# Input projections of a hybrid-attention encoder: 512 columns at a time and weight parts in nine single tiles

## The chip, the cores and the metric

The kernel runs on one core of one Trainium2 chip. The metric is the device time of one execution in microseconds, from the first to the last instruction with what lies around it. Before the change three runs took 2704.49, 2706.41 and 2711.77 us (median 2706.41). Engine names are those of the profile: PE is TensorE (matmuls; PEld its weight loads), DVE is VectorE, ACT is ScalarE, POOL is GpSimd, SP is the engine whose queue issues the DMAs.

## The reference, cut to what matters

```python
D_MODEL = 1024; SEQ = 2048; HEAD_DIM = 64       # 8 + 8 heads, D_FF = 4096, all float32
def reference(x, c, g_norm1, w_in, g_q, g_k, rel_bias, w_o, g_norm2, w1, w2, w_ada, b_ada):
    ...
    mod = c_act @ w_ada[l] + b_ada[l]
    sh1, sc1, gt1, sh2, sc2, gt2 = [m[:, None, :] for m in jnp.split(mod, 6, axis=-1)]
    h = rmsnorm(x, g_norm1[l]) * (1.0 + sc1) + sh1
    proj = h @ w_in[l]
    q_sb, k_sb, v_sb, q_ca, k_ca, v_ca = jnp.split(proj, split_pts, axis=-1)
    ...
    q_ca = rmsnorm(hs(q_ca, N_CA_HEADS), g_q[l])
    k_ca = rmsnorm(hs(k_ca, N_CA_HEADS), g_k[l])
    ...
    x = x + gt1 * (mixed @ w_o[l])
    h = rmsnorm(x, g_norm2[l]) * (1.0 + sc2) + sh2
    x = x + gt2 * (jnp.square(jax.nn.relu(h @ w1[l])) @ w2[l])
```

The change lies in `proj = h @ w_in`: a product of 2048 x 1024 by 1024 x 3072. Its columns are six kinds of 512: q, k, v of the eight stick-breaking heads ("sb") and q, k, v of the eight chunked-attention heads ("ca"). The q and k of the second group also get an RMS norm over each head's 64 columns.

## The kernel before

Products in full precision are made of three fast ones: each operand is split in a high and a low part (`split`, line 146: ACT copies the high part, DVE or POOL subtracts it for the low part), and `mm3` (202) adds high x high, high x low and low x high. Tokens are taken in reverse, in four blocks of 512 (tb 3, 2, 1, 0).

The program has three stages. The first makes most of the projections, and on the side the 48 columns of `mod`, the prepared bias, and the split parts of w_o and of some of w_in, which it stores to DRAM for later. The second is the attention, into which the remaining projections and the output projection are filled. The third is the MLP, made of seven products per pair of blocks. Only the first is touched.

*Pieces and jobs.* w_in is cut into 12 pieces of 256 columns: 0 to 5 are q, k, v of sb, 6 to 11 those of ca. A job (f, piece, tb) is one piece for one block of tokens; its first number tells loads of the same piece apart. The list `jobs` (521 to 524) has 31. Pieces 0 to 3 use weights as the stationary operand and 512 tokens as the moving one (tiles `pq`): two blocks of 24 matmuls of 512 columns. The others use 128 tokens as the stationary operand and the 256 columns of the piece as the moving one (tiles `pt`): 96 matmuls in two blocks, a bank of PSUM holding two groups of 128 tokens. `project` (309) issues a job, and gives way after each block, so that `run_job` (535) can put side work behind it.

*Behind a block.* Values (pieces 4, 5, 10, 11) are split and stored. For q and k of ca, ACT squares the bank (`csq`), DVE sums per head (`cv`), POOL takes the inverse root (`rsqrt`, 150), and DVE multiplies the bank by it (`scale`, 346, writes `qh`), which frees the bank. When all four groups of 128 tokens are there, TensorE turns them (`turn`, 356, tiles `px`), and ACT and DVE split and store them.

*What sets the order.* TensorE always runs in program order; so do ACT, DVE, POOL and SP from job 7 on (`Ordered`, 34; `ORDERED`, 532), while up to there a scheduler orders these four. `Later` (57) holds closures that run a number of ticks later, one tick per block: `later` for `scale` and `turn`, `norms` for the three parts of a block's norm, `behind` for stores and the second halves of side work. Side work `todo` (527 to 530) has costs: 1.5 for a column of `mod` (`ada`: a load `wa` of 512 KB, two ticks later `ada_column` on DVE), 1.8 for a bias, 4.4 for a part of w_o (`prepare_wo`). Every block earns credit (573): 3.0 in early jobs of q, k of ca, 2.2 from job 7 on.

*Norms.* `start_norm(tb, wait)` (401) squares eight x tiles on ACT and adds them on DVE (`nsaa`); after `wait` ticks `norm_rstd` (171) makes eight small matmuls (`pva`), DVE `nva`, POOL the root, DVE `ndga`; some ticks later `norm_spread` makes `pra` and DVE scales x. `end_norm` (417) then makes the operand tiles `ht` of the block: per x tile two operations on ACT and one on DVE.

*Buffers.* PSUM banks come from `Banks` (253), which hands out in turn z, z, ps, z, z, ps: four buffers of tag z, two of tag ps. Raw weights come into `ring` (three of 8 KB a partition). Split weights lie in `wp` (251): two tiles `wh` and two `wl` of a whole piece, so a piece is split while the one before it is in use. `load_w` (281) splits with four pool subtractions per piece, in the ordered part at given points (`parts`). `stp` (250) has six staging tiles of 4 KB, `adaw` four for `wa`, `xp` ten x tiles.

Of the kernel before, what the change touches and what calls it, by code (L numbers as in the profile page):

```python
# [79 lines left out]
def encoder_kernel(ctx, tc, xT, c, g1, g2, w_in, gqk, bias, w_o, w1, w2, w_ada, b_ada, out):  # L80
# [127 lines left out]
    def store_qk(kind, ca, ps, pl, pair, tb, nm, g=None):  # L208
        st = pl.tile([P, 2, TB], F32R, tag="st", name=f"st{nm}")
# [27 lines left out]
    SBQK, CAQK, VALS = (2, 3, 0, 1), (6, 7, 8, 9), (4, 5, 10, 11)  # L237

    pa, er = ctx.enter_context(ExitStack()), ctx.enter_context(ExitStack())
    if True:
        xp = er.enter_context(tc.tile_pool(name="xp", bufs=KT + 2, side="right"))
        adaw = er.enter_context(tc.tile_pool(name="adaw", bufs=4, side="right"))
        adap = er.enter_context(tc.tile_pool(name="adap", bufs=1, side="right"))
# [4 lines left out]
        stp = pa.enter_context(tc.tile_pool(name="stp", bufs=6))  # L250
        wp = pa.enter_context(tc.tile_pool(name="wp", bufs=2))
# [3 lines left out]
        cb = adap.tile([P, D], F32, name="cb")  # L255
        cg = adap.tile([P, D], F32, name="cg")
# [8 lines left out]
        parts = []  # L265
# [10 lines left out]
        def load_raw(half, piece, q=None):  # L276
            wr = ring.tile([P, KT, CW], F32, tag="r8", name=f"wr{half}_{piece}")
            (q or sp).dma_start(wr, w_in[piece])
            return wr

        def load_w(half, piece, q=None, wr=None, parts=None):

            if wr is None:
                wr = load_raw(half, piece, q or sp)
            wh = wp.tile([P, KT, CW], F32R, tag="wh", name=f"wh{half}_{piece}")
            wl = wp.tile([P, KT, CW], F32R, tag="wl", name=f"wl{half}_{piece}")

            def low(k):
                pool.tensor_tensor(wl[:, k], wr[:, k], wh[:, k].bitcast(F32), op=ALU.subtract)

            for k in (slice(0, KT // 2), slice(KT // 2, KT)):
                act.copy(wh[:, k], wr[:, k])
                for kk in (slice(k.start, k.start + 2), slice(k.start + 2, k.stop)):
                    if parts is None:
                        low(kk)
                    else:
                        parts.append(lambda kk=kk: low(kk))
            if parts is not None:
                parts.append(lambda: behind.add(2, lambda: keep_w(half, piece, wh, wl)))
            elif q is None:  # L300
                keep_w(half, piece, wh, wl)
            return wh, wl

        def keep_w(half, piece, wh, wl):
            if half in (0, 2) and piece not in CAQK:
                for l, w in enumerate((wh, wl)):
                    sp.dma_start(scr_w[piece,][:, :, l, :], w.bitcast(F32))

        def project(piece, tb, ht, wh, wl):

            grp, hf = divmod(piece, 2)
            kind, ca = grp % 3, grp // 3
            nm = f"{piece}_{tb}"
            if not ca and kind < 2:
                for n in range(2):
                    ps = pp.tile([P, TB], F32, tag="ps", name=f"pq{nm}_{n}")
                    cl = slice(n * P, (n + 1) * P)
                    for k in range(KT):
                        mm3(ps, wh[:, k, cl], wl[:, k, cl], ht[k][:, 0, :], ht[k][:, 1, :], k == 0, k == KT - 1)
                    store_qk(kind, 0, ps, stp, hf * 2 + n, tb, f"{nm}_{n}")  # L320
                    yield
                return
            if kind < 2:
# [1284 lines left out]
```

## Time and profile before

| | before |
|---|---|
| median of three runs | 2706.41 us |
| profiled execution, its own time | 2706.24 us |
| its span, first to last instruction | 2704.4 us |
| instructions | 42721 |
| mean granted TensorE clock | 0.992 |
| 0 to 74 us: PE, DVE, ACT, POOL busy; DMA share | 51.9, 48.5, 40.1, 41.1 us; 0.93 |
| 436 to 1500 us | 1007.5, 857.3, 775.4, 645.7 us; 0.75 |
| 1500 to 2704 us | 1196.2, 798.6, 570.2, 206.0 us; 0.61 |

How to read it: rows of the timeline give the start in us, the length, the engine, the operation with its tiles (out<-in, numbers left out), the shape and how many were merged; in brackets stands the idle time before it and what ended that. Rows by stage give the length of the stretch, then for each engine its busy time and the number of instructions, the granted clock, the busy share of the DMA engines and GB/s. Rows of groups give busy time and the mean ns of one, then the idle time before them. L42 is the wrapper that keeps program order, so instructions are told apart by tile. Matmuls overlap: one lasts longer than the distance to the next, so their pace is read from starts.

### The profile page before, as it was taken

How to read it: one execution, taken by the hardware profiler on the slowest of the kernel's cores; microseconds unless marked ns; L12 is line 12 of the kernel's file. 1: busy time of each engine (PE TensorE's matmuls, PEld its weight loads, DVE VectorE, ACT ScalarE, POOL GpSimd, SP SyncE). 2: the span in 40 equal slices, each digit the busy share in tenths (PEclk: the TensorE clock that was granted, in tenths of full speed). 3: DMA queues.
4: the chain of work that ended last, by engine and by line, in shares of the span. 5: the costliest groups of instructions: out<-in, count | busy, mean ns of one | idle time of the engine just before them, and what ended most of it. 6: DMA issues, size and time to landing. Idle time of an engine off the chain costs nothing. (4 is left out here: it accounts for less than half of the span.)

```text
span 2704.4 us, 42721 instructions
## 1 busy us (share of the span) xinstructions
PE 2616.3 (97%) x14192; PEld 2231.1 (82%) x14192; DVE 1885.4 (70%) x3159; ACT 1516.7 (56%) x2926; POOL 1065.6 (39%) x1296
## 2 busy tenths in 40 slices
PE   6999999899999999999998999999999999999999
PEld 5899998778778987778876788878888888888887
DVE  6435555688789878989756777768866565655565
ACT  5423445687688878878643444455644444444443
POOL 5464365566466656767533323202001323200000
PEclk9999999999999999999999999999999999999999
DMA  9869977878888687756766876786675444465574
GB/s 341 314 253 341 379 276 232 259 245 256 267 258 245 210 262 250 231 190 207 215 227 215 283 265 254 266 334 210 230 265 186 150 152 152 148 238 190 202 265 156
DMA packets 265579, 650.36 MB, mean 240 GB/s; under 512 B 29200, under 2 KB 65040, under 8 KB 255632
## 3 DMA queue, kind: packets, MB, share of 16 engines
q1 hardware_dynamic: 264576, 645.55, 70.0%
q10 hardware_dynamic: 784, 2.10, 0.3%
q8 instruction: 112, 1.84, 0.3%
q14 instruction: 107, 0.88, 0.1%
HBM read 456.16 MB, written 191.37 MB: 239 GB/s over the span
## 5 line engine op out<-in xcount | busy, mean ns | idle before, releaser
L42 PE MATMUL ps<-oph,opv 128*128 128x512 f32 x2688 | 613.0, 390 | 1.6 <-ACT opv L42 1.5
L42 PE MATMUL ps<-h,opw 128*128 128x512 f32 x2664 | 605.1, 390 | 2.7 <-DVE cx L42 2.7
L42 PEld LDWEIGHTS ps<-oph,opv 128*128 128x128 f32 x2688 | 505.5, 188 | 107.1 <-ACT opv L42 1.9
L42 PEld LDWEIGHTS ps<-h,opw 128*128 128x128 f32 x2664 | 499.9, 188 | 107.6 <-DVE cx L42 3.9
L42 POOL TENSOR_TENSOR b<-b,p 128x512 f32<-128x512 f32 (+1 forms) x320 | 359.7, 1124 | 189.1 <-DVE p L42 168.5
L42 DVE TENSOR_TENSOR wtl<-wt,wth 128x512 fp32r<-128x512 f32 (+3 forms) x544 | 290.5, 545 | 51.3 <-ACT wth L42 49.1
L42 ACT CAST wth<-wt 128x512 fp32r<-128x512 f32 (+3 forms) x544 | 257.5, 484 | 119.5 <-PE wt L42 104.2
L42 DVE TENSOR_TENSOR oph<-hw,oph 128x512 fp32r<-128x512 f32 x224 | 160.6, 717 | 214.0 <-ACT oph L42 213.9
L42 PE MATMUL pt<-wh,ht 128*128 128x256 f32 x1664 | 304.3, 284 | 1.3 <-DVE qh L42 1.3
L42 ACT CAST oph<-hw 128x512 fp32r<-128x512 f32 x224 | 139.3, 622 | 290.4 <-PE ps L42 274.1
L42 DVE TENSOR_TENSOR_SCAN p<-z,p,zero 128x512 f32<-128x512 f32 x192 | 246.1, 1282 | 33.9 <-ACT z L42 28.6
L42 PEld LDWEIGHTS pt<-wh,ht 128*128 128x128 f32 x1664 | 261.0, 192 | 1.6 <-ACT st L42 1.5
L42 POOL TENSOR_TENSOR ts<-w 128x512 f32<-128x512 f32 x32 | 45.2, 1413 | 547.2 <-DMA w<-in_w_dram 490.9
L42 PE MATMUL pt<-wl,ht 128*128 128x256 f32 x832 | 235.7, 283 | 0.0
L42 PE MATMUL acc<-wth,v 128*128 128x512 f32 (+3 forms) x544 | 223.1, 414 | 0.8 <-ACT e L42 0.8
L42 ACT ACTIVATE b<-z 128x512 f32<-128x512 f32 (+1 forms) x320 | 171.5, 536 | 63.3 <-PE z L42 46.6
L42 POOL TENSOR_TENSOR e<-e,cols 128x640 f32<-128x640 f32 (+4 forms) x128 | 142.9, 1120 | 147.1 <-DVE cols L42 90.3
L42 PE MATMUL z<-k,q 128*128 128x512 f32 (+3 forms) x640 | 186.2, 372 | 9.9 <-DVE p L42 7.2
L42 PE MATMUL acc<-wtl,v 128*128 128x512 f32 (+3 forms) x544 | 187.7, 351 | 0.0
L42 PE MATMUL wt<-ident,b 128*128 128x128 f32 x1088 | 172.6, 274 | 6.7 <-DVE cols L42 5.0
L42 DVE TENSOR_TENSOR opw<-w,opw 128x512 fp32r<-128x512 f32 x127 | 95.3, 752 | 115.4 <-ACT opw L42 115.3
L42 ACT ACTIVATE z<-z 128x512 f32<-128x512 f32 (+1 forms) x320 | 170.6, 533 | 0.0
(222 smaller groups left out, 4700.3 us busy)
## 6 DMA issues: line engine op xcount, KB each, us to landing
hw<-scr_hid SPq DMA_DIRECT2D x112, 512.0 KB, 3.9
v<-scr_v SPq DMA_DIRECT2D x136, 256.0 KB, 3.9
k<-scr_k SPq DMA_DIRECT2D x268, 128.0 KB, 4.2
w<-in_w_dram SPq DMA_DIRECT2D x64, 512.0 KB, 5.2
hw<-scr_s SPq DMA_DIRECT2D x64, 512.0 KB, 4.7
q<-scr_q SPq DMA_DIRECT2D x124, 256.0 KB, 5.2
fw<-scr_w SPq DMA_DIRECT2D x28, 1024.0 KB, 7.1
wa<-in_w_ada_dram SPq DMA_DIRECT2D x48, 512.0 KB, 7.2
```

The lines of the kernel that those rows point to most:

```text
L42: return lambda *x, **y: self.tc.keep_in_program_order(f(*x, **y))
```

## The change

Pieces 4 to 11 are taken in pairs. A key is now one of the pieces 0 to 3 (256 columns) or a whole kind of 512 columns, named by its even piece (4, 6, 8, 10), which comes from a second input `w_rest` (the same numbers of w_in, laid out by 512 columns, in two raw tiles of four k-tiles each). A job of such a key has four blocks, one for each 128 tokens, of 24 matmuls of 512 columns, each in a bank of its own. The list has 18 jobs. Piece 3 is now read and split twice (keys (0,3) and (2,3)).

The split weights lie in nine tiles of 4 KB a partition, each high and low part of one k-tile (or of two k-tiles of a 256-column piece). While the last block of a key's last job runs, each k-tile's tile is free after its three matmuls, and the next key's next part is made into it (`pump`): ACT copies; POOL subtracts for pieces 0 to 3, DVE for the others. Split parts go to DRAM part by part (64 stores of 256 KB instead of 16 of 1 MB). Staging tiles are three of 8 KB, each holding two blocks or pairs of heads. `scale` runs two ticks later, the four `turn`s at three and four ticks. The norms start and end at other blocks (`hook`). `ada_column` writes its products over its input.

```diff
-        wp = pa.enter_context(tc.tile_pool(name="wp", bufs=2))
+        stp = pa.enter_context(tc.tile_pool(name="stp", bufs=3))
+        wp = pa.enter_context(tc.tile_pool(name="wp", bufs=WT))
...
-            dve.tensor_tensor_reduce(cb, wa, cs, 1.0, bcol[:, j : j + 1], ALU.mult, ALU.add, m)
+            dve.tensor_tensor_reduce(wa, wa, cs, 1.0, bcol[:, j : j + 1], ALU.mult, ALU.add, m)
...
+        def weight_parts(key, m):
+            f, p = key
+            w = w_tile(f"{f}_{p}_{m}")
+            wts.setdefault(key, []).append(w)
+            if p < 4:
+                src = raws[key, 0][:, 2 * m : 2 * m + 2, :]
+                hi, lo = (w[:, l, :].rearrange("p (k c) -> p k c", c=CW) for l in range(2))
+            else:
+                src = raws[key, m // 4][:, m % 4, :]
+                hi, lo = w[:, 0, :], w[:, 1, :]
+            split(hi, lo, src, pool if p < 4 else dve)
+            if f == 2:
+                for l, x in enumerate((hi, lo)):
+                    behind.add(2, lambda l=l, x=x: sp.dma_start(scr_w[p,][:, 2 * m : 2 * m + 2, l, :], x.bitcast(F32)))
+            if f == 0 and p in VALS:
+                for c in range(2):
+                    behind.add(
+                        2 + m // 4,
+                        lambda c=c: sp.dma_start(
+                            scr_w[p + c,][:, m, :, :], w[:, :, c * CW : (c + 1) * CW].bitcast(F32)
+                        ),
+                    )
...
+        def pump():
+            while coming and free[0]:
+                weight_parts(*coming.pop(0))
...
+            for tt in range(4):
+                ps = pp.tile([P, TB], F32, tag="ps", name=f"pt{nm}_{tt}")
+                tl = slice(tt * P, (tt + 1) * P)
+                if last and tt == 3:
+                    pump()
+                for k in range(KT):
+                    mm3(ps, ht[k][:, 0, tl], ht[k][:, 1, tl], *weight_of(key, k), k == 0, k == KT - 1)
+                    if last and tt == 3:
+                        free[0] += 1
+                        pump()
...
-                later.add(2 if osp is sp else 1, scale)
-                if t2 == 1:
+                later.add(2, scale)
+                if tt == 3:
...
-                    later.add(4, lambda: turn(0))
-                    later.add(4, lambda: turn(1))
+                    for n in range(4):
+                        later.add(3 + n // 2, lambda n=n: turn(n))
...
-        jobs = [(0, 3, 3), (0, 6, 3), (0, 3, 2), (0, 6, 2), (2, 2, 2), (0, 0, 2), (0, 1, 2)]
-        jobs += [(0, p, t) for p in seq[5:10] for t in (3, 2)]
-        jobs += [(0, 10, 3), (0, 11, 3), (0, 10, 2), (0, 11, 2)]
-        jobs += [(1, p, t) for p, t in ((4, 1), (6, 1), (7, 1), (6, 0), (7, 0), (8, 1), (8, 0), (9, 1), (9, 0), (5, 1))]
+        jobs = [(0, 3, 3), (0, 6, 3), (0, 6, 2), (2, 3, 2), (2, 2, 2), (2, 0, 2), (2, 1, 2)]
+        jobs += [(0, p, t) for p in (8, 4, 10) for t in (3, 2)]
+        jobs += [(1, p, t) for p, t in ((6, 1), (6, 0), (8, 1), (8, 0), (4, 1))]
...
-        start_norm(2, 1)
+        start_norm(2, 2, 2)
+
+        def hook(job, n):
+            if (job, n) == ((0, 6, 3), 2):
+                norms.flush()
+                end_norm(2, h_tile(2))
+                load_x(1)
+            if (job, n) == ((0, 4, 3), 0):
+                start_norm(1, 5, 3)
+            if (job, n) == ((0, 10, 2), 0):
+                norms.flush()
+                end_norm(1, h_tile(1))
+                load_x(0)
+                behind.add(3, lambda: start_norm(0, 2, 1))
+            if (job, n) == ((1, 6, 1), 2):
+                norms.flush()
+                end_norm(0, h_tile(0))
+            if (job, n) == ((1, 6, 0), 1):
+                sp.dma_start(scr_h, whole[0].bitcast(F32))
...
+            load_raws()
+            if last and key != keys[-1]:
+                after = keys[keys.index(key) + 1]
+                coming.extend((after, m) for m in range(len(wts.get(after, ())), count[after]))
+            bank = project(key, t, hts[t], last)
+            for b in range(2 if key[1] < 4 else 4):
+                hook(jobs[n], b)
                 next(bank)
                 behind.tick()
                 norms.tick()
                 later.tick()
-                credit += 2.2 if n >= ORDERED else 3.0 * (p in CAQK)
+                credit += 2.2 if n >= ORDERED else 3.0 * (key[1] in CAQK)
```

`load_raws` keeps up to three raw tiles ahead of the parts made from them. The second and third arguments of `start_norm` are the ticks to its second part (`pva`) and from there to its third (`pra`).

More of the change, by code (lines that the diff above doesn't have):

```diff
@@ L274, in affine @@
             dve.scalar_tensor_tensor(aff[:, which, :], sc, 1.0, gcol[:, which, :], op0=ALU.add, op1=ALU.mult)
[L276 to L314, printed above, removed]
+        raws, wts, free = {}, {}, [WT]
+        def load_raw(key, m, q=None):
+            p = key[1]
+            if p < 4:
+                raws[key, 0] = ring.tile([P, KT, CW], F32, tag="r8", name=f"wr{key[0]}_{p}")
+                src = w_in[p]
+            else:
+                raws[key, m] = ring.tile([P, KT // 2, TB], F32, tag="r8", name=f"wr{key[0]}_{p}_{m}")
+                src = w_rest[p // 2 - 2][:, m * KT // 2 : (m + 1) * KT // 2, :]
+            (q or sp).dma_start(raws[key, m], src)
@@ L315, in project @@
+        def project(key, tb, ht, last):
+            f, piece = key
+            nm = f"{f}_{piece}_{tb}"
+            if piece < 4:
+                kind, hf = divmod(piece, 2)
                 for n in range(2):
@@ L399, in load_x, with start_norm @@
                 xts[tb].append(xt)
-        def start_norm(tb, wait=3):
+        def start_norm(tb, wait, more):
             tg = f"a{tb}"
@@ L411, in third @@
                         dve.tensor_tensor(x, x, r, op=ALU.mult)
-                norms.add(3 if wait > 3 else min(2, wait), third)
+                norms.add(more, third)
             norms.add(wait, second)
```

167 lines of the change are left out of this document (80 added, 87 removed).

## The prediction

> **What bounds the kernel now.** I read the page's busy shares first, then the busy time by stage, then who waits for whom, then the order of time.
>
> ```profile
> PE 2616.3 (97%) x14192; PEld 2231.1 (82%) x14192; DVE 1885.4 (70%) x3159; ACT 1516.7 (56%) x2926; POOL 1065.6 (39%) x1296
> ```
> ```profile
> core 0: us, PE busy (x) PEld busy (x) DVE busy (x) ACT busy (x) POOL busy (x), PEclk, DMA share, GB/s
> 74.00:436.00 362.00, 360.71 (x2849) 352.66 (x2847) 181.15 (x293) 131.03 (x195) 172.78 (x249) 1.00 0.83 304
> ```
>
> TensorE is busy 97% of the span. The changed code runs in this stretch (its last job ends a little later): 362 us, of which TensorE is busy 360.7 at a granted clock of 1.00. DVE is busy 181 us there, ACT 131, POOL 173, and the DMA engines 0.83 of the time. So the stage is as long as TensorE's stream, and only two things can change the total: the pitch of the matmuls, and waits of TensorE that appear or go. The waits (engine, tile <- releaser: total us, times, longest) say how few there are:
>
> ```profile
> PE pva L42 <- DVE nsaa L168: 2.1, 1, 2.1
> PE pt L42 <- DVE qh L42: 1.3, 1, 1.3
> ```
>
> From 64 us, where the projections of the first job begin, to the stage's end TensorE waits twice, 2.1 and 1.3 us. Everybody else is ahead of it.
>
> **The pitch.** The timeline gives it best by first and last starts (start us, length, engine, operation, count).
>
> ```profile
> 91.10 0.39 PE L42 MATMUL pq<-ht,wl 128*128 128x512 f32 x1
> ...
> 96.54 0.39 PE L42 MATMUL pq<-ht,wl 128*128 128x512 f32 x1
> ...
> 239.77 0.28 PE L42 MATMUL pt<-wl,ht 128*128 128x256 f32 x1
> ...
> 245.53 0.28 PE L42 MATMUL pt<-wl,ht 128*128 128x256 f32 x1
> ```
>
> The last two rows lie 48 matmuls of 256 columns apart: 5.76 us, 120.0 ns each, though one lasts 280 ns (they overlap). The first two lie 24 matmuls of 512 columns apart: 5.44 us, 226.7 ns. In the job list 26 jobs of 96 narrow matmuls (2496) become 13 of 96 wide ones (1248). A wide one replaces two narrow ones: 240.0 - 226.7 = 13.3 ns, times 1248 = **16.6 us gained**. With tokens as weights at 512 columns nothing runs yet; the bounds are 0 (240 ns, the old pair) and the 16.6 of the two rows. I take the upper end: the same 128x128 stationary shape and 512 columns, only the roles change. A block of 24 such matmuls then takes 5.44 us, and a job of a whole kind 21.8.
>
> [...]
>
> **Weight parts.** Per key of 512 columns the parts are eight ACT copies and eight subtractions, now on DVE instead of POOL.
>
> ```profile
> L42 ACT CAST ht<-xt 128x512 fp32r<-128x512 f32 x16 | 9.9, 620 | 0.5
> L42 DVE TENSOR_TENSOR ht<-xt,ht 128x512 fp32r<-128x512 f32 x16 | 11.0, 691 | 8.9 <-ACT ht L42 8.8
> ```
>
> Nearest rows, the same shapes in the norm: 0.62 us on ACT, 0.69 on DVE. Seven keys put 56 x 0.69 = 39 us on DVE, on 181 of 362: covered by the idle half. What is new is when they run. With nine tiles and eight in use, part m waits until the last block is through with tile m-1; it is ready 1.3 us (0.62 + 0.69) later and needed 5.44 us after that tile came free, so the handover has about 4 us of slack. Where ACT and DVE are free it costs nothing; where other work stands ahead of it in their order, TensorE waits.
>
> **Four places where it does.** (Blocks of a job count from 0.) (a) A job with a head norm needs a bank per block; `scale`, the last reader, is issued one block after its own, and behind that block's square and reduce. By the fixed row of banks (4 of tag z, 2 of tag ps, taken z z p), counting allocations in TensorE's order, blocks 1, 2 and 3 of jobs (0,8,2) and (1,6,0) all fall on ps. So block 3 waits for the `scale` of block 1, which is issued after block 2. The old trace holds this sequence, without anyone waiting for it:
>
> ```profile
> 183.87 1.04 PE L42 MATMUL px<-ident,qh 128*128 128x128 f32 x8
> 184.66 0.36 PE L42 MATMUL pt<-wh,ht 128*128 128x256 f32 x1
> ...
> 208.63 1.03 PE L42 MATMUL px<-ident,qh 128*128 128x128 f32 x8
> ```
> ```profile
> 185.50 1.40 DVE L42 SCALAR_TENSOR_TENSOR st<-px,gqk_s,st 128x512 fp32r<-128x512 f32 x2
> 186.82 0.68 DVE L42 TENSOR_TENSOR qh<-pt,cy 128x512 f32<-128x512 f32 x1
> ...
> 212.78 0.68 DVE L42 TENSOR_TENSOR qh<-pt,cy 128x512 f32<-128x512 f32 x1
> ```
>
> TensorE's block ends at 183.87, its transposes `px` take it to 184.66, and DVE ends the `scale` (`qh`) at 187.50: 2.8 us after TensorE would go on. With one `ada_column` in between (208.63 + 0.79 to 213.46) it is 4.0. By the credits (24 from the two early jobs, then 2.2 a block) (0,8,2) has none there, (1,6,0) one: **2.8 and 4.0 us lost**. Bounds: 0, if POOL and DVE are quicker than the old order says, and 5.2 each with one more column (1.2 more again). A gain is excluded: nothing is taken away.
>
> (b) `start_norm(0)` is now issued after block 2 of (0,10,2), its second part (`pva`) after block 3 instead of three blocks on, and its third (`pra`) after one block more. Block 3 is also where key (1,6) is split, behind the sums and a `prepare_wo`.
>
> ```profile
> 288.06 0.59 ACT L42 CAST sv<-pt 128x512 fp32r<-128x512 f32 x1 [3.54 <-PE pt L42]
> ...
> 305.83 0.64 ACT L42 ACTIVATE nsaa<-xt 128x512 f32<-128x512 f32 x1
> ...
> 315.73 1.05 ACT L42 CAST woh<-wo 128x1024 fp32r<-128x1024 f32 x1 [3.70 <-DMA wo<-in_w_o_dram]
> ```
> ```profile
> 307.01 5.47 DVE L42 TENSOR_TENSOR nsaa<-nsaa,nsqa 128x512 f32<-128x512 f32 x7 [0.36 <-ACT nsqa L42]
> ...
> 316.81 1.23 DVE L42 TENSOR_TENSOR wol<-wo,woh 128x1024 fp32r<-128x1024 f32 x1 [0.91 <-ACT woh L42]
> ...
> 319.80 0.15 DVE L42 TENSOR_SCALAR nva<-pva 128x4 f32<-128x4 f32 x1
> 322.57 1.75 DVE L42 TENSOR_TENSOR ndga<-ident,nya 128x512 f32<-128x512 f32 x1 [2.62 <-POOL nya L42]
> ```
> ```profile
> 71.41 0.69 DVE L183 TENSOR_TENSOR ndga<-ident,nya 128x512 f32<-128x512 f32 x1 [2.59 <-POOL nya L156]
> ```
> ```profile
> 297.29 6.49 SPq L42 DMA_DIRECT2D xt<-in_xT_dram  x8
> ...
> 308.22 1.24 SPq L42 DMA_DIRECT2D wo<-in_w_o_dram  x1
> ```
>
> Count from the start of (0,10,2), in the old trace just before 288.06. Block 2 ends at 16.3, the squares start at 17.0 and the last add ends 6.65 us later (305.83 to 312.48): 23.7. TensorE was ready for `pva` at 21.8. The x loads left SP at 9.2 to 15.7; the raw w_o tile stands right behind them now, issued at 16 and landed 7.5 later (308.22 to 315.73): 23.5, its two operations (1.05, 1.23) end at 25.9, the first part is ready at 26.6. TensorE, 0.8 us of `pva` done (eight small matmuls, like the `px` above), has waited **4.0 us**. DVE then makes a part per 0.69 (to 31.4), the block's value part (0.69), `nva` (0.15) at 32.3; POOL takes it to 34.9 (319.95 to 322.57) and `ndga` 0.7 more, as at 71.41: 35.6. Block 0 of (1,6,1) ended at 32.0: **3.6 us lost** at `pra`. Together 7.6; bounds 1.9 (only the sums late) and 13 (transfers 5.4 us, a block, later than then).
>
> (c) `start_norm(1)` sits at the head of (0,4,3); its 6.65 us push the last `scale` of (0,8,2) to about 11.8 us after the handover, the transposes come after two blocks, 10.9: 0.9 lost, between 0 and 4.
>
> **The start.** `pva` of token block 2 moves behind the second block of (0,3,3), so the 2.1 us should go. In exchange (0,6) must be split by DVE, 8 x 0.69 = 5.5 us.
>
> ```profile
> 60.00:74.00 14.00, 11.86 (x59) 9.72 (x58) 7.44 (x10) 5.25 (x9) 7.66 (x9) 1.00 1.05 376
> 220.00:340.00 120.00, 120.00 (x1006) 120.00 (x1006) 72.16 (x105) 48.70 (x72) 43.57 (x51) 1.00 1.04 381
> ```
>
> DVE idles 6.6 of the 14 us there, so I count 2.1 gained; bounds 2.1 gained and 5.5 lost. The wait of 1.3 I count as gone, since the second half of `end_norm(0)` now has two blocks behind it; else 0.
>
> **The sum**, on the profiled execution's own 2706.24 us (span 2704.4; the median, 2706.41, is the same within 0.01%): -16.6 - 2.1 - 1.3 + 2.8 + 4.0 + 7.6 + 0.9 = -4.7, **2701.5 us**. The two later stages issue the same work.
>
> **Rivals.** *The waits don't come* (banks free sooner, transfers early): 2706.2 - 20.0 = 2686.2. For it: TensorE waited for nothing here before. Against: the orders of (a) and (b) are fixed in the code.
>
> *The DMA takes over*, slower. From 220 to 340 the row above shows the engines full, at 381 GB/s. The bytes stay, plus a second read of piece 3 (1.05 MB), but TensorE asks 5.5% faster, and 4 MB of split weights leave in two blocks, just ahead of the w_ada loads on which DVE already waits:
>
> ```profile
> DVE cb L42 <- DMA wa<-in_w_ada_dram: 10.6, 5, 4.3
> ```
>
> If the stretch keeps its length, 120 us x 13.3/240 = 6.6 is lost again, the reread takes 2.8, and one burst of 4.19 MB, 11.0 us at 381 GB/s, ends in a DVE wait ahead of a handover: 2701.5 + 20.4 = 2721.9. It decides once DVE's wait there passes the 4 us of slack; today the longest is some 4. Against it: a wait of 10.6 us in all reached TensorE nowhere.
>
> [...]
>
> *The pitch stays* (240 ns): 2718.1. [...] *The start, left to the scheduler, comes out badly*: 2.1 + 5.5 more, 2709.1.
>
> **How the numbers follow.** Some 0.3%, 8.1 us, is what a measurement tells from no change: faster is below 2698.3, slower above 2714.5. The forecast has 0.45, its own range 2694 to 2709 (the bounds of (b) and one of (a)); 0.18 of it lies on the faster side. No waits 0.24, all faster. DMA 0.20, of which 0.18 slower. Pitch 0.05, slower. [...] Start 0.06, of which 0.02 slower. Faster 0.18 + 0.24 = 0.42; slower 0.18 + 0.05 + 0.02 = 0.25; the same 0.33. The range, 2685 to 2722, runs from the first rival to the second and leaves out about 0.16.
>
> **What would show it.** Right: `pt` x1248 at 226.7 ns from first to last starts; TensorE's waits in this stage some 15 us, named by `qh` in (0,8,2) and (1,6,0), by `nsaa`, weight parts and `ndga` around (1,6,1). Wrong: a pitch near 240; fewer than 8 us of waits (then it is nearer 2686); waits on weight parts at every change of key, or DVE waiting tens of us for `wa` (then DMA, and slower).

## The result, and the profile after

| | before | after |
|---|---|---|
| median, runs | 2708.72 us, 6 | 2734.50 us, 6 |
| lowest to highest | 2704.49 to 2714.52 us | 2733.39 to 2737.15 us |
| ratio after / before, 95% interval | | 1.0096 (1.0082 to 1.0110) |
| profiled execution | 2706.24 us, span 2704.4 us | 2737.15 us, span 2735.4 us |
| first `pt` to first `pf` (see below) | 74.27 to 440.81 us | 71.48 to 466.40 us |

The change makes the kernel about 26 us slower, 1.0%. The forecast was 2701.5 us in a range of 2685 to 2722: wrong in sign and in size, and outside the range.

Where the time went is found with two landmarks: the first matmul of the projections with tokens as weights (`pt`), and the first one that the attention stage fills in (`pf`). The second comes 25.6 us later than before (466.40 against 440.81), which is nearly the whole difference of the medians (25.8). The two later stages issue the same work; in these two executions they took 2269.0 and 2263.6 us, and across the runs below 2260.7 to 2272.3. One row for the stretch between the landmarks, before and after (length; then for each engine busy time and instructions; granted clock, DMA share, GB/s):

```profile
74.27:440.81 366.54, 363.39 (x2867) 354.59 (x2865) 185.15 (x298) 135.00 (x204) 173.28 (x250) 1.00 0.83 305
```
```profile
71.48:466.40 394.92, 365.29 (x1625) 297.61 (x1625) 208.45 (x349) 142.54 (x236) 112.43 (x207) 0.96 0.79 288
```

TensorE was idle for 3.1 us of this stretch before and for 29.6 after, and its granted clock, 1.00 before, has a mean of 0.96. So there are two losses: waits, and matmuls that run at a lower clock. The waits are rows of the TensorE timeline of after, with the idle time before each and what ended it (rows with waits under 0.6 us are left out, and one of 1.31 us in the attention's first matmuls, where before has one of 1.52):

```profile
115.49 7.30 PE L42 MATMUL pt<-w,ht 128*128 128x512 f32 x24 [2.90 <-DVE qh L392]
...
159.57 0.73 PE L42 MATMUL pq<-ht,w 128*128 128x512 f32 x2 [0.99 <-ACT w L147]
160.93 10.95 PE L42 MATMUL pq<-ht,w 128*128 128x512 f32 x40 [0.62 <-POOL w L148]
...
186.14 32.54 PE L42 MATMUL pt<-w,ht 128*128 128x512 f32 x129 [7.08 <-ACT w L147]
228.63 18.20 PE L42 MATMUL pt<-w,ht 128*128 128x512 f32 x72 [2.74 <-DVE qh L42]
...
332.10 1.84 PE L42 MATMUL pva<-ones,nsaa 128*128 128x1 f32 x8 [5.20 <-DVE nsaa L42]
...
382.80 18.34 PE L42 MATMUL pt<-w,ht 128*128 128x512 f32 x72 [4.59 <-DVE qh L42]
...
450.27 0.77 PE L42 MATMUL px<-ident,qh 128*128 128x128 f32 x5 [1.70 <-DVE qh L42]
```

2.74, 5.20 and 4.59 us are the waits that the prediction named, at its places. 2.90 and the ones on weight parts (`w`; 10.6 us with the small ones between) it did not have. The first and last of the projections at the new width, and their durations:

```profile
L42 PE MATMUL pt<-w,ht x1248: 387/390/797, 71.5 to 462.4; 128*128 128x512 f32 x179
```
```profile
295.69 31.21 PE L42 MATMUL pt<-w,ht 128*128 128x512 f32 x137
```

137 matmuls in 31.21 us, of which the last lasts 0.39: 30.82 / 136 = 226.6 ns from start to start. The pitch is the predicted one. The longest matmul, 797 ns, lasts twice the median: half clock. When that comes is best seen by cutting the timeline at the moments at which the clock changes, here around the wait that ends at 228.63 (same columns as the first rows; the granted clock is the third number from the end):

```profile
226.06:229.48 3.42, 0.85 (x4) 0.75 (x5) 2.99 (x6) 1.25 (x3) 2.54 (x3) 1.00 1.01 402
229.48:232.89 3.41, 3.41 (x10) 2.67 (x9) 1.50 (x3) 1.85 (x3) 0.40 (x2) 0.50 1.00 308
232.89:236.30 3.41, 3.41 (x17) 2.80 (x16) 2.97 (x5) 2.81 (x5) 0.00 (x0) 1.00 1.05 402
```

TensorE is busy for 0.85 of 3.42 us; in the next 3.41 us it is fully busy, starts 10 matmuls where it could start 17, and then it is at full clock again. In after the clock falls to 0.50 at 116.84, 161.21, 181.69, 229.48, 331.88 and 379.66 us. The first and the last lie 262.82 us apart, which is 77 steps of 3.413 us; all the distances between these times are whole multiples of that, to 0.02 us (44.37 is 13 of them, 215.04 is 63), and the halved stretches last 3.41, 6.83 or 10.24 us: in this trace the clock changes on a grid. TensorE is busy for 26.3 us of the halved windows, so it does 13.2 us less work in them than at full clock.

The stretch of after so is 394.92 = 352.1 + 29.6 idle + 13.2 at half clock, and that of before 366.54 = 363.4 + 3.1 + 0. The stream itself became 11.3 us shorter, the start 2.8 us earlier, and 39.7 us of waits and their clock came in: -11.3 - 2.8 + 26.5 + 13.2 = 25.6.

### The profile page after: what moved, and what is told of

Same layout as the page of the kernel before. It is cut to its first block, busy times and chain, and to the rows that moved or that the text cites. A ratio compares the mean times of both kernels' runs of the same rounds, so it can differ in the third digit from the quotient of the medians.

```text
span 2735.4 us, 40253 instructions
## 1 busy us (share of the span) xinstructions
PE 2622.0 (96%) x12944; PEld 2175.4 (80%) x12944; DVE 1922.0 (70%) x3215; ACT 1527.2 (56%) x2966; POOL 997.4 (36%) x1244
## 5 line engine op out<-in xcount | busy, mean ns | idle before, releaser
L42 PE MATMUL pt<-w,ht 128*128 128x512 f32 x1248 | 301.0, 402 | 19.3 <-ACT w L147 8.1
L42 PEld LDWEIGHTS pt<-w,ht 128*128 128x128 f32 x1248 | 239.1, 193 | 73.7 <-issue 10.9
L42 PE MATMUL po<-fx,ow 128*128 128x512 f32 x576 | 167.4, 406 | 4.7 <-DMA ow<-scr_wo 4.7
```

The lines of the kernel that those rows point to most:

```text
L42: return lambda *x, **y: self.tc.keep_in_program_order(f(*x, **y))
```

## The experiments

Each was run beside the kernel before, on the chip that it ran on (medians of before 2707.4 to 2709.0, so medians of different rows compare to within 1 or 2 us). For each, the profiled execution gives the stretch between the landmarks, TensorE's idle time in it, the work lost at half clock (TensorE's busy time in a window of 3.413 us times one minus its clock, summed), and what remains. From all2 on the rows are combinations; the six edits are those of `banks` with the later turns, `early`, `vals`, the stores of pieces 0 and 1 from the first tile, and less side work.

| run | median us | ratio to before (95%) | stretch | idle | half clock | rest |
|---|---|---|---|---|---|---|
| before | 2708.72 | | 366.5 | 3.1 | 0.0 | 363.4 |
| after | 2734.50 | 1.0096 (1.0082 to 1.0110) | 394.9 | 29.6 | 13.2 | 352.1 |
| hold | 2717.21 | 1.0037 (1.0024 to 1.0050) | 380.4 | 21.9 | 8.4 | 350.0 |
| early | 2726.96 | 1.0067 (1.0046 to 1.0089) | 385.5 | 23.4 | 11.5 | 350.6 |
| spread | 2749.79 | 1.0144 (1.0122 to 1.0166) | 411.7 | 42.4 | 18.1 | 351.1 |
| wide1 | 2728.55 | 1.0079 (1.0060 to 1.0098) | 387.4 | 25.6 | 10.8 | 351.1 |
| banks | 2736.82 | 1.0102 (1.0087 to 1.0117) | 399.2 | 32.2 | 14.7 | 352.3 |
| banksturn | 2727.53 | 1.0076 (1.0059 to 1.0093) | 388.5 | 27.6 | 8.9 | 352.0 |
| quiet | 2734.03 | 1.0092 (1.0077 to 1.0108) | 398.7 | 31.3 | 15.7 | 351.7 |
| vals | 2732.86 | 1.0091 (1.0074 to 1.0108) | 393.7 | 29.2 | 12.3 | 352.2 |
| all2 | 2717.91 | 1.0041 (1.0026 to 1.0056) | 378.7 | 18.9 | 8.7 | 351.1 |
| all3 | 2723.89 | 1.0063 (1.0046 to 1.0081) | 381.6 | 24.1 | 7.3 | 350.2 |
| all4 | 2717.21 | 1.0036 (1.0023 to 1.0049) | 375.9 | 19.2 | 6.4 | 350.3 |
| all5, six edits | 2706.16 | 0.9993 (0.9981 to 1.0005) | 366.6 | 10.9 | 5.1 | 350.5 |
| nobank | 2720.78 | 1.0042 (1.0030 to 1.0054) | 381.0 | 23.4 | 8.1 | 349.5 |
| noquiet | 2710.85 | 1.0013 (1.0005 to 1.0022) | 370.4 | 16.0 | 2.9 | 351.5 |
| all6 | 2706.34 | 0.9989 (0.9978 to 1.0001) | 364.0 | 9.9 | 3.4 | 350.7 |
| all7 | 2720.34 | 1.0045 (1.0033 to 1.0057) | 379.0 | 21.5 | 6.8 | 350.7 |
| all8 | 2704.36 | 0.9988 (0.9978 to 0.9999) | 361.5 | 10.9 | 0.0 | 350.6 |
| all9 | 2707.64 | 1.0002 (0.9991 to 1.0012) | 370.2 | 13.3 | 6.4 | 350.4 |

The last column is the result that carries the rest: in nineteen kernels with the wide matmuls, whose stretches differ by 50 us, it lies between 349.5 and 352.3. The stage is TensorE's stream plus TensorE's idle time plus the half-clock loss, and nothing else of size.

### A weight tile is held by its own store

On ACT's timeline of after, the copies that make the parts wait for the stores to DRAM; on SP's, these stores' issue (start, length, count) shows that they are slow to leave:

```profile
158.90 0.62 ACT L147 CAST w<-wr 128x512 fp32r<-128x512 f32 x1 [6.49 <-DMA scr_w<-w]
...
185.47 0.62 ACT L147 CAST w<-wr 128x512 fp32r<-128x512 f32 x1 [7.92 <-DMA scr_w<-w]
```
```profile
148.84 8.97 SPq L306 DMA_DIRECT2D scr_w<-w  x8
...
176.09 8.29 SPq L306 DMA_DIRECT2D scr_w<-w  x8
```

Four keys in a row, (2,3), (2,2), (2,0) and (2,1), store 2 MB each, in a stretch in which the DMA engines are full (share 1.04 from 170 to 190 us). A tile comes free for the next key when its matmuls are done *and* its store has read it. Four experiments:

`hold` lets the same stores read other data, so that the weights of pieces 0 to 3 never reach DRAM:

```diff
-                    behind.add(2, lambda l=l, x=x: sp.dma_start(scr_w[p,][:, 2 * m : 2 * m + 2, l, :], x.bitcast(F32)))
+                    behind.add(2, lambda l=l, x=x: sp.dma_start(scr_w[p,][:, 2 * m : 2 * m + 2, l, :], whole[2][:, 2 * m : 2 * m + 2, l, 0:CW].bitcast(F32)))
```

> The changed kernel with one edit: the stores of the split parts of pieces 0 to 3 to DRAM read as many bytes from the h tile of token block 2 instead of from the weight tiles (what they store is then not the weights). Bytes, count and queue of the transfers are the same; only the weight tiles are no longer held by them. Theory H (a weight tile can't be refilled while its own store still reads it): ACT's waits on the scr_w stores between 141 and 189 us go, with them TensorE's 10.6 us of waits from 159 to 186 us and 4.6 us of half clock: about 15 us, 2719. Rival B (the DMA engines are full there, raw weights would be late anyhow): the waits stay within 3 us of 10.6 and are named by raw weights; 2732 or more.

2717.21 us, 17.3 less than after. TensorE's timeline at the same place has no wait left:

```profile
140.80 27.46 PE L42 MATMUL pq<-ht,w 128*128 128x512 f32 x120
168.10 32.81 PE L42 MATMUL pt<-w,ht 128*128 128x512 f32 x144
```

Bytes, queue and count of the transfers were the same; SP issues them within 0.3 us of the same times as in after, and the DMA engines are as full (share 1.04 from 170 to 190 us in both). So it is the hold, not the full DMA engines, that made TensorE wait (theory H). 3.7 us of waits on `qh` stand at the transposes at 202 to 205 us instead.

`early` issues the stores one tick sooner:

```diff
-                    behind.add(2, lambda l=l, x=x: sp.dma_start(scr_w[p,][:, 2 * m : 2 * m + 2, l, :], x.bitcast(F32)))
+                    behind.add(1, lambda l=l, x=x: sp.dma_start(scr_w[p,][:, 2 * m : 2 * m + 2, l, :], x.bitcast(F32)))
```

> The changed kernel (2734.5 us) with one edit: the stores of the split parts of pieces 0 to 3 are issued one tick, a block of 5.44 us, sooner. Theory H (the tile is held by its own store, so a store that leaves a block sooner frees the tile a block sooner): the waits on weight parts from 159 to 190 us go from 10.6 us to 3 or less, with the half clock after them, as in the run where the stores read elsewhere (2717.2): 2717 to 2721. Rival B (the DMA engines are full there, 0.99 to 1.04, so issuing sooner lands no sooner): half of the waits or more stay, 2728 or more.

2726.96 us: 7.5 less, between the two theories. The waits on parts shrink from 10.6 to 4.6 us (1.84, 0.22, 1.91 and 0.63 at 172 to 182), so a sooner issue frees the tiles sooner, but not by a whole block. The rest has two sources on ACT's timeline: ahead of the first of these waits it stands 2.77 us for raw weights, ahead of the later ones 3.21 and 1.95 us for stores. Why these land late is not shown.

`spread` moves (0,8,3) and (0,8,2) between the four storing keys:

```diff
-        jobs = [(0, 3, 3), (0, 6, 3), (0, 6, 2), (2, 3, 2), (2, 2, 2), (2, 0, 2), (2, 1, 2)]
-        jobs += [(0, p, t) for p in (8, 4, 10) for t in (3, 2)]
+        jobs = [(0, 3, 3), (0, 6, 3), (0, 6, 2), (2, 3, 2), (2, 2, 2), (0, 8, 3), (0, 8, 2), (2, 0, 2), (2, 1, 2)]
+        jobs += [(0, p, t) for p in (4, 10) for t in (3, 2)]
```

> The changed kernel with one edit in the order of jobs: (0,8,3) and (0,8,2) come between (2,2,2) and (2,0,2), so that the four keys which store 2 MB each are two and two, with eight blocks between. Theory H: half or more of the 10.6 us of waits on weight parts and of the 4.6 us of half clock go, 8 to 15 us: 2720 to 2727. Rival B (the same bytes in the same stage, so the lateness only moves): 2732 to 2737. The waits named by qh stay or change place, since the row of banks meets the jobs in another phase.

Worse than both theories allowed: 2749.79 us. The timeline shows why:

```profile
160.20 31.47 PE L42 MATMUL pt<-w,ht 128*128 128x512 f32 x129 [8.02 <-ACT w L147]
...
231.87 0.69 PE L42 MATMUL pt<-w,ht 128*128 128x512 f32 x1 [2.58 <-ACT w L42]
...
242.06 26.02 PE L42 MATMUL pt<-w,ht 128*128 128x512 f32 x105 [4.57 <-ACT w L42]
```

The wait sits where a storing key hands over to a key of eight parts; now this happens twice, and ACT waits for stores both times (10.52 and 7.50 us). Two storing keys in a row are enough for a wait of 8.02 us, so it is this handover that costs, and not the run of four keys. Of the 12.8 us that TensorE is idle longer, some 5 are at the two handovers; the rest came later, at `pva` (8.47 us), at `pra` and at other parts.

`wide1` takes the store of the last of them away. The tile `wide`, in which the first block's projections keep pieces 0 and 1, has the split parts already:

```diff
-            if f == 2:
+            if f == 2 and p not in (1,):
...
+        for p in (1,):
+            osp.dma_start(scr_w[p,], wide[:, :, :, p, :].bitcast(F32))
```

> The changed kernel (2734.5 us) with one edit: the split parts of piece 1 go to DRAM at 65 us or so from the tile in which the first token block's projections have them already; key (2,1) stores nothing, so its tiles are not held when key (0,8) is to be split. Theory H: the waits on weight parts at the handover to (0,8), 7.08 and 1.9 us in small pieces, go, with 3 us of half clock; 1.6 us at 159 us stay: about 12 us, 2722. Rival E (2 MB more in the first 90 us make x or raw weights of (0,6) late): waits of TensorE before 120 us grow by 5 us or more, 2727 or more.

2728.55 us, 5.9 less than after. The 7.08 went (1.4 us in four pieces are left at that handover), but 1.6 us before it became 2.58, and `pva` waited 7.50 us in place of 5.20: nearly half of what was won was lost at the next meeting places.

### The bank wait: real, but not alone

```diff
             for tt in range(4):
+                if kind != 2 and tt == 3 and pp.homes[0][1] == "ps":
+                    pp.homes[0], pp.homes[1] = pp.homes[1], pp.homes[0]
                 ps = pp.tile([P, TB], F32, tag="ps", name=f"pt{nm}_{tt}")
```

> The changed kernel (2734.5 us) with one edit: block 3 of a job of q or k of ca takes a z bank where the row of banks would hand it ps. Theory W (waits plus clock): the three waits of TensorE named by qh (2.90, 2.74 and 4.59 us, at 115, 228 and 382 us) go, and with each of them the stretch at half clock that follows it, 1.7 to 1.9 us of lost work each: 10.2 + 5.3 = 15.5 us, so about 2719. Rival P (a wait costs its own length, the low clock has another cause): 10.2 us, 2724, and the half-clock stretches stay. Rival M (the late scale only moves the wait to the transposes px): 2730 or more, with px waiting on qh.

2736.82 us: nothing gained (rival M). The three waits are gone from their places and stand one step on, at the transposes that need the same late `scale`, and at `pva`:

```profile
136.15 1.33 PE L42 MATMUL px<-ident,qh 128*128 128x128 f32 x5 [3.04 <-DVE qh L394]
...
336.46 1.84 PE L42 MATMUL pva<-ones,nsaa 128*128 128x1 f32 x8 [8.39 <-DVE nsaa L42]
...
401.84 1.31 PE L42 MATMUL px<-ident,qh 128*128 128x128 f32 x5 [1.91 <-DVE qh L42]
...
454.97 1.33 PE L42 MATMUL px<-ident,qh 128*128 128x128 f32 x5 [4.16 <-DVE qh L42]
```

`banksturn` moves the second meeting place too, beside the edit of `banks`:

```diff
-                        later.add(3 + n // 2, lambda n=n: turn(n))
+                        later.add(4 + n // 2, lambda n=n: turn(n))
```

> The changed kernel with two edits: block 3 of a job of q or k of ca takes a z bank where the row would give ps, and the four turns come one tick later (four and five). Theory L (scale on DVE is late by some 2 to 4 us; TensorE meets it at the bank or, with the bank free, at the transposes): with both places moved out of the way the waits named by qh fall from 11.9 us (changed kernel) and 10.3 us (banks alone) to 3 or less, the rest stays: 2720 to 2727. Rival S (the stage is paced by DMA and DVE, and TensorE that comes sooner waits longer at the next meeting place, pva and weight parts): those grow by what the qh waits lose, 2732 to 2738.

2727.53 us, 7.0 less than after: the waits named by `qh` fall from 11.9 to 0.2 us, and a wait on parts of 4.13 and a longer `pva` (7.60) take some of it. Theory L and rival S are both partly right.

### The late norm of the last block

In after the first part of that norm came 5.20 us late. DVE's and SP's rows show a chain that the prediction did not have:

```profile
316.27 1.28 DVE L42 CUSTOM_DVE_ANT_0 wa<-wa,cs,bcol 128x1024 f32<-128x1024 f32 x1 [7.57 <-DMA wa<-in_w_ada_dram]
317.48 4.90 DVE L42 TENSOR_TENSOR ht<-xt,ht 128x512 fp32r<-128x512 f32 x8
...
322.90 1.27 DVE L42 CUSTOM_DVE_ANT_0 wa<-wa,cs,bcol 128x1024 f32<-128x1024 f32 x1
...
324.70 1.27 DVE L42 CUSTOM_DVE_ANT_0 wa<-wa,cs,bcol 128x1024 f32<-128x1024 f32 x1
...
326.50 5.45 DVE L42 TENSOR_TENSOR nsaa<-nsaa,nsqa 128x512 f32<-128x512 f32 x7
```
```profile
303.00 6.89 SPq L42 DMA_DIRECT2D scr_w<-w  x8
310.20 0.34 SPq L42 DMA_DIRECT2D wa<-in_w_ada_dram  x1
...
314.86 8.29 SPq L42 DMA_DIRECT2D xt<-in_xT_dram  x8
```

SP is 6.89 us at eight stores of weight parts; a load of w_ada leaves behind them; DVE stands on it for 7.57 us; behind that stand the subtractions that free the x tiles, behind these the loads of block 0's x, and behind them its sums. The two columns of `mod` directly ahead of the sums (322.90 and 324.70) add to it: the second square was ready at about 324.6 us on ACT's timeline, and the sums began at 326.50. Two edits, each against one end of the chain. `quiet`:

```diff
-                credit += 2.2 if n >= ORDERED else 3.0 * (key[1] in CAQK)
+                if jobs[n] != (0, 10, 2) and (jobs[n], b) not in (((0, 10, 3), 2), ((0, 10, 3), 3)):
+                    credit += 2.2 if n >= ORDERED else 3.0 * (key[1] in CAQK)
```

> The changed kernel with one edit: no side work is begun in the last two blocks of (0,10,3) and in (0,10,2); it comes in later blocks. Theory D (the 5.20 us wait for pva goes back to DVE: it stands 7.57 us on a load of w_ada, the subtractions of end_norm(1) stand behind that, the x tiles come free late, their next loads are late, and the sums with them): the wait falls to 2 us or less and the half clock after it (3.3 us of lost work) goes: about 6.5 us, 2728. Rival F (the place of the sums in program order alone sets it): the wait stays at 4 to 5 us, 2733 or more.

2734.03 us, no gain. The edit did not do what it was to do: credit left from before still began one column there, and DVE stood 7.48 us on that one. The wait for `pva` was 3.26. `vals` spreads the stores:

```diff
                     behind.add(
-                        2 + m // 4,
+                        1 + m // 2,
```

> The changed kernel with one edit: the sixteen stores of the split parts of a key of values leave four to a block in four blocks, from one tick after the first part, instead of eight to a block in two. Theory D (SP stands some 7 us at a time on these stores, a load of w_ada is issued late behind them, DVE stands 7.6 us on it, end_norm(1) and the sums behind that): DVE's longest wait on a w_ada load in (0,10,2) falls below 4 us and the wait for pva from 5.20 us to 3 or less, with the half clock after it: 5 us or so, 2729. Rival F (the place of the sums in program order sets it): 4 us or more stay, 2733 or more.

2732.86 us; DVE's longest wait on such a load there was 4.81 us and `pva` waited 3.17 us, both just short of what theory D asked for. 1.6 us are within what the runs scatter, so nothing is decided by the time.

### Together, and each left out

`all2` is `early`, `banksturn` and `vals` in one.

> The changed kernel with the edits of the three runs beside this one together: sooner stores of pieces 0 to 3, a z bank for block 3, turns one tick later, and the stores of values spread over four blocks. If each wait has a cause of its own (theories H, L, D): -15 - 10 - 5 us, about 2704, level with the kernel before or a little under it. Rival S (the stage is paced by DMA and DVE): 2715 or more, with TensorE's waits in the stage still above 20 us.

2717.91 us, 16.6 less than after (the three alone: 7.5, 7.0 and 1.6). What is left at 164 to 178 us is another lateness: ACT waits 7.71 us for the second half of key (0,8)'s raw weights, which SP issued behind four stores. `all3` adds the edit of `wide1`:

> The edits of the four together (2717.9 us) and that of piece 1. Theory H: the 6.28 + 1.99 us at the handover to (0,8) go, with 4 us of half clock: 2706 to 2709, level with the kernel before. Rival S (TensorE that comes sooner waits longer at the next meeting place): pva and the parts of (1,6) take 5 us or more of it, 2712 or more.

2723.89 us, 6.0 more than all2. TensorE is idle for 5.2 us more. A wait of 4.22 us at 123.31, named by `st`, is 3.2 longer than the two that all2 has there; its cause was not followed up. `pva` waits 1.9 longer, a wait on parts is 1.0 shorter, and the handover costs 1.3 more: ACT now waits 9.72 us for that same load, issued at 172.08, in the part in which a scheduler orders SP. `all4` adds a `quiet` that does what it says, at the head of the lines that give credit and begin side work:

```diff
+                if jobs[n] == (0, 10, 2) or jobs[n] == (0, 10, 3) and b > 0:
+                    continue
                 credit += 2.2 if n >= ORDERED else 3.0 * (key[1] in CAQK)
```

> As the run beside it, and no side work is begun from block 1 of (0,10,3) to the end of (0,10,2). Theory D (DVE's wait on a w_ada load, behind which end_norm(1) stands, makes the sums of block 0 late): no such wait is left there, the wait for pva falls below 1.5 us and the half clock after it goes, 5 to 7 us: about 2701, faster than the kernel before. Rival F (the place of the sums in program order sets it): pva waits 3 us or more, no gain.

2717.21 us, 6.7 less. `pva`:

```profile
320.72 1.02 PE L42 MATMUL pva<-ones,nsaa 128*128 128x1 f32 x8 [1.89 <-DVE nsaa L42]
```

6.37 in all3, 1.89 here, as theory D has it, but not for the whole of its reason. DVE still stands 7.64 us on a load of w_ada that was begun before; gone are a second such wait (4.80 in all3) and the columns' own time ahead of the subtractions and the sums. The chain itself is borne out: in all3 ACT's first square of block 0 waits 4.27 us for x, here it does not wait for x. Which share the loads have and which the columns' own time, no run separates. What is left fits the place of the sums in program order (the prediction's lower bound for this place was 1.9). `all5` stores pieces 0 and 1 both from `wide` (`(0, 1)` for `(1,)` in the edit of `wide1`):

> As the run beside it, with pieces 0 and 1 both stored from the first tile, 4 MB before 95 us. If the DMA engines have room there (0.71 and 0.57 busy from 70 to 110 us in the changed kernel): within 2 us of the run beside it or 2 us faster, since key (2,0) holds no tile either. If not: the second token block's operands, which go into the tile that is being stored, are late, TensorE waits 4 us or more before 100 us, and it is 5 us or more slower than the run beside it.

2706.16 us, 11.1 less than all4 and level with before. The expectation allowed for 2 us: the wait of 9.69 us at the handover to (0,8) is gone with the last two stores that held tiles, and the one of 4.22 is 1.97. Now edits of the six are taken out again: in `nobank` those of the bank row and the turns, in `noquiet` that of the side work.

> The six edits together (2706.2 us) less two: bank row and turns as in the changed kernel again. Theory L (the bank wait has a cost of its own, since scale stands one block behind in program order): waits of 2.7 to 4.6 us named by qh come back at two or three places, with half clock after most of them, 8 to 14 us: 2714 to 2720. Rival S (meeting places of one lateness, and that is gone): within 3 us of 2706.

2720.78 us, 14.6 more (theory L). The waits are back, and with them, here, one of 6.41:

```profile
116.42 5.73 PE L42 MATMUL pt<-w,ht 128*128 128x512 f32 x24 [3.04 <-DVE qh L392]
...
216.61 18.20 PE L42 MATMUL pt<-w,ht 128*128 128x512 f32 x72 [2.74 <-DVE qh L42]
...
365.15 16.61 PE L42 MATMUL pt<-w,ht 128*128 128x512 f32 x72 [2.75 <-DVE qh L42]
435.59 1.33 PE L42 MATMUL px<-ident,qh 128*128 128x128 f32 x5 [6.41 <-DVE qh L42]
```

The two edits that returned 7.0 us alone (`banksturn`) are worth 14.6 us as the last of the six.

> The six edits together (2706.2 us) less one: side work is begun in (0,10,3) and (0,10,2) again. Theory D (a w_ada load in DVE's order makes end_norm(1), the x loads and the sums late): the wait for pva goes from 1.88 to 4 us or more and half clock follows, 4 to 7 us: 2710 to 2713. Rival S: within 2 us of 2706.

2710.85 us, 4.7 more (the two intervals in the table just meet, at 1.0005); `pva` waits 6.66 us, and ACT's first square again 4.50 us for x.

The last four try what is left: `all6` is all5 with the last norm one tick later, `all7` is all6 with the engines in program order from job 3 on, and `all8` and `all9` are all6 and all5 with less side work in the two jobs of key (0,6):

```diff
-                behind.add(3, lambda: start_norm(0, 2, 1))
+                behind.add(4, lambda: start_norm(0, 2, 1))
...
-        ORDERED = 7
+        ORDERED = 3
...
-                credit += 2.2 if n >= ORDERED else 3.0 * (key[1] in CAQK)
+                credit += 2.5 if n >= ORDERED else 2.0 * (key[1] in CAQK)
```

> The six edits together (2706.2 us) and a seventh: the norm of block 0 starts one tick later, so that pva stands behind block 0 of (1,6,1) and the parts of key (1,6) come ahead of its sums. If its place in the order is what is left of that wait: the 1.88 us and the half clock after it go, 2 to 4 us, 2703. Rival: pra or block 0's operands are late instead (end_norm(0) now has the third part of the norm directly ahead of it), TensorE waits 3 us or more on ht before (1,6,0): 2708 or more.

> The run beside it with ACT, DVE, POOL and SP in program order from job 3 on instead of job 7. If the waits from 120 to 170 us (1.97, 0.52 and 2.37 us, named by qh and st) come from the order that the scheduler chose: they shrink to 2 us together, 3 to 5 us, 2699. If they come from the amount of work there: the same within 2 us, or weight parts wait behind stores in the fixed order and it is slower by 3 us or more.

> The seven edits (2706.3 us) and less side work in the jobs of key (0,6): credit 2.0 a block there in place of 3.0, 2.5 from job 7 on in place of 2.2. If the waits from 120 to 170 us (1.97, 1.14, 1.89) come from DVE's columns and w_o parts standing ahead of scale and the store splits: 3 us or more of them go, with 1.7 us of half clock, 2701 or so. If not, or if the side work makes the later jobs late instead: 2706 or more.

> The six edits (2706.2 us) with the same change of side work: by the first reason 2701 or so, by the second 2706 or more; against the run beside it the shift of the norm of block 0 is worth 0 to 2 us, as between the six and the seven.

2706.34, 2720.34, 2704.36 and 2707.64 us. The shift left 1.88 us at `pva` and changed nothing that can be told. Program order from job 3 brings waits on parts of 5.32 and 6.35 us: the scheduler's order was the better one. Less early side work changed nothing that can be told (2.0 less with the shift, 1.5 more without). The best version, all8, is at 0.9988 (0.9978 to 0.9999) of before, which is hardly more than level with it.

## Why the prediction was wrong

*The pitch: right.* 226.6 ns where 226.7 was said; the rival with 240 ns falls away. But the rest of the stretch, idle time and clock taken off, is 349.5 to 352.3 us where 363.4 - 16.6 = 346.8 should stand: 2.7 to 5.5 us of the gain are missing, 5.3 in after. Two parts can be read from the traces. Eight `pra` matmuls that came ahead of the first `pt` before (0.8 us) now lie in the stretch. And the last matmul before a wait counts as busy for its whole 0.39 us, not for its pitch of 0.23; after has 16 waits of 0.1 us or more, some 2.6 us. About 2 us stay open.

*The start: right.* The wait of 2.1 us is gone. Of the 2.8 us that the first `pt` came earlier, 0.8 are those eight `pra`; and this start scatters, from 71.1 to 74.3 us over the nineteen kernels that share it. *(a): right in place, size and cause* (2.74 and 4.59 for 2.8 and 4.0), but not complete: (0,6,2) has the same row of banks, ps for its blocks 1, 2 and 3, and waited 2.90 us. The prediction looked only at the ordered jobs. *(b): right in place, near in size by luck* (5.20 for 4.0 at `pva`, nothing for 3.6 at `pra`), wrong in its chain: not the raw w_o but the w_ada load, behind stores on SP, and columns of `mod` ahead of the sums. *(c)*: none came in (0,4,3).

*The step that failed first* is under "Weight parts": "the handover has about 4 us of slack. Where ACT and DVE are free it costs nothing". It counted a tile free when its matmuls are through with it. The tile of a storing key is also read by its own store, which is issued two ticks after the part, when the key's last block begins, and which takes up to 9 us to leave SP. ACT and DVE were idle there; the copy waited for the store. That was 10.6 us of waits and 4.6 of half clock in after, and 17.3 us by the run that lifts it. The rival "the DMA takes over" had the sign, but put the burst at the keys of values, from 220 to 340 us, and let it act through DVE; it came at 150 to 190, through the tiles.

*The second failed step* is the price of a wait, taken as its length everywhere. Waits that make up 24.1 of the 29.6 us (2.90, 0.99 + 0.62, 7.08, 2.74, 5.20, 4.59) were followed by half clock, 13.2 us of lost work in all. The kernel before has two waits in this stage, 2.1 and 1.3 us, and a clock of 1.00: nothing in its profile showed this price in this stage, but elsewhere in it the clock was below 1 (0.992 over the whole), and that was not followed up.

*The sum by its terms:* -16.6 became -11.3; the start -2.8; waits at the named places 12.5 us (2.74, 5.20, 4.59) against 15.3; waits at places not named 15.8 (2.90, 10.6, 1.70 and 0.53 at `px`); half clock 13.2, which the prediction put at nothing. *The signs to look for* were partly right: the waits of `qh` and `nsaa` came as named, and "waits on weight parts" were named as the sign of a DMA bound; they came at two handovers (1.6 and 9.0 us), not at each.

## What to carry to other kernels

A buffer's hold ends with its last reader, and a store is a reader (here its hold cost 17.3 us, by `hold`): when buffers are cut finer and handed over one by one, list for each the store that still reads it, when that is issued, and what stands ahead of it in its queue. Waits that have one source are met one after the other, so an edit that removes one can return less alone (7.0 us for bank row and turns, nothing for the bank row without the turns) than as the last of six (14.6 us); judge it with the others gone, and by what TensorE waits for next. And price a wait of TensorE above its length: here 29.6 us idle cost 42.8.

## What the runs showed of the hardware

*The clock falls after short waits, on a grid.* In the eighteen traces with a halved window in this stage (after and all experiments but all8), the falls of one trace lie on one grid of 3.413 us, whose phase differs from run to run. Windows at full clock between 71 and 480 us, by TensorE's idle time in them, and the window after:

| idle in the window of 3.413 us | windows | next at half clock |
|---|---|---|
| 0.4 to 1.0 us | 58 | 0 |
| 1.0 to 1.6 us | 46 | 4 |
| 1.6 to 1.9 us | 20 | 8 |
| 1.91 us and more | 61 | 61 |

The four in the second row all hold `pva`, eight matmuls of one column, which count as busy time (0.95 us for such a row in after, at 265.01). The trace of all8 has one exception: on the grid of its falls at 31.61 and 502.65 us, the window from 376.36 holds 1.95 us of idle time and no halved window follows. So in these traces, but for that one window, a wait was dear wherever it left TensorE 1.50 us of work or less in a window of 3.41 and in 8 of 20 windows with 1.5 to 1.8 us, and a wait as long as a dear one could straddle a line and cost only itself. In `hold` the bank wait of 2.74 us, which cost a halved window in after, did so:

```profile
211.73:215.14 3.41, 2.14 (x14) 1.66 (x12) 1.45 (x4) 2.11 (x4) 0.44 (x1) 1.00 0.90 363
215.14:218.56 3.42, 1.96 (x9) 1.64 (x10) 2.25 (x5) 1.06 (x3) 2.50 (x5) 1.00 1.01 331
218.56:221.97 3.41, 3.41 (x17) 2.81 (x16) 3.40 (x6) 3.10 (x6) 0.00 (x0) 1.00 1.01 385
```

In after one wait of 2.74 us (0.85 us busy in 226.06 to 229.48), and two of 0.99 and 0.62 us in one window (1.81 us busy in 157.79 to 161.21), were enough for a halved window.

*It may make times scatter.* In the profiled execution of all8 the longest of the waits is 2.67 us, cut by a line into 1.95 and 0.72, and no window of the stretch was halved:

```profile
72.67:434.16 361.49, 350.61 (x1625) 289.73 (x1625) 208.11 (x349) 139.30 (x236) 112.04 (x207) 1.00 0.84 309
```

That execution took 2696.72 us, the shortest of its eleven; the longest took 2710.31. The record gives the granted clock of every execution, and in each kernel's runs the longer executions have the lower clock on the whole (correlation -0.49 over these eleven, -0.48 to -0.84 over the 19, 21 and 23 of before). That the grid's phase makes this difference fits, but only one execution of each kernel has a trace, so it is not shown.
